# Hybrid decoder layer: the gated linear unit as seven products of quarters, with the merge of its first half placed behind five of the last seven

## The chip, the cores and the metric

The kernel runs on one core of a Trainium2 chip. Its time is the device time of one execution in microseconds (us); lower is better. The engines are PE (TensorE, matrix products), ACT (ScalarE), DVE (VectorE), POOL (GpSimd) and SP (SyncE, which issues most DMA transfers). Each engine works through its own queue in order.

## The reference, cut to what matters

```python
y = s5_ssm(u, ...)                                   # (1, 1040, 1024)
z = jax.nn.gelu(y)
za, zb = jnp.split(z @ w_glu[i], 2, axis=-1)         # w_glu: 1024 x 2048
ssm = za * jax.nn.sigmoid(zb)
merged = (jax.nn.sigmoid(g_att) * rmsnorm(attn, attn_branch_norm[i])
          + jax.nn.sigmoid(g_ssm) * rmsnorm(ssm, ssm_branch_norm[i]))
h = h + merged @ w_out[i]
hn = rmsnorm(h, norm_ffn[i])
gate, up = jnp.split(hn @ w_ffn_in[i], 2, axis=-1)
h = h + (jax.nn.silu(gate) * up) @ w_ffn_out[i]
```

The sequence has 1024 tokens behind 16 prepended ones, the width is 1024, the FFN's inner width 2816. All is float32.

## The kernel before, in words

A float32 product is made of three passes over parts: each operand is split into a high part (cast by ACT to fp32r) and a low part (the difference, on DVE or, for weights read by `w_cols`, on POOL, L104), and `PASSES` gives high x high, high x low, low x high. One "product" below is one matmul instruction of 128 x 128 by 128 x 512.

The stages around the change follow each other. First come the gate projections (`g_unit`), with the attention branch scaled by its gate and written to `pa_d`; beside them DVE runs the scan of the state space branch. Then the z stage: for each of eight blocks of 128 channels three loads (`uty`, `tp`, `ct`, three buffers each), 16 products of 128 columns into `y`, a gelu on ACT into `z`, eight transpositions by PE into `zT`, and the split of these into `zt[h]`, high and low, for the two halves `h` of the tokens. The gated unit follows: for each of eight blocks `f` of output channels and each half, `cols_unit` makes 24 products for `za` and 24 for `zb`; ACT takes the sigmoid, DVE multiplies and applies the gate `gs`, and squares are summed into `acc[h]`. The first half of all blocks, and the second of the first six, come ahead of `merge(0)` in the code; the second halves of blocks 6 and 7 ("late") come after, then `merge(1)`. `merge(h)` makes the root mean square from `acc[h]` (a reduction on PE, `ssq_ssm`; 13 small operations of DVE; four products and a copy, `rsb_ssm`), multiplies the eight blocks, adds the attention branch `mpa` (on POOL) and splits the sum into `mt[h]`. Then `w_out`: two column halves `n`, eight token blocks `b`, 24 products each into `wo`, of which `b` < 4 need `mt[0]` and the others `mt[1]`; DVE adds the residual (`h`, L984), which frees the bank. The FFN behind it already uses seven products of quarters (Strassen's scheme in Winograd's form), with `mixed` making the mixed quarters t2, t1, t4 of its input.

The program is recorded in the order of the code, and the library's scheduler then sorts the instructions of each engine by a timeline it models, within what dependencies and buffers allow. So the order on an engine is not the code's; it is read from the built program. Eight banks hold PE's results, under the tags m (2), s (2), x (3) and q (1).

## Time and profile before

| | |
|---|---|
| median of three runs | 1691.5 us (1687.93 to 1700.41) |
| profiled execution, its own time | 1697.95 us |
| its span in the trace | 1696.2 us |
| mean granted clock of TensorE | 0.975 |
| PE busy | 1586.7 us, 94% |
| DVE busy | 1181.0 us, 70% |
| ACT busy | 695.7 us, 41% |
| POOL busy | 372.4 us, 22% |

The profile is of one execution, so its rows add up to the profiled time and not to the median. The share of PE is a mean over stages: an engine with a low share overall can set the end of one stage. A matmul row's duration is modelled; the distance between the starts of rows tells the pace.

### The profile page before, as it was taken

How to read it: one execution, taken by the hardware profiler on the slowest of the kernel's cores; microseconds unless marked ns; L12 is line 12 of the kernel's file. 1: busy time of each engine (PE TensorE's matmuls, PEld its weight loads, DVE VectorE, ACT ScalarE, POOL GpSimd, SP SyncE). 2: the span in 40 equal slices, each digit the busy share in tenths (PEclk: the TensorE clock that was granted, in tenths of full speed). 3: DMA queues.
4: the chain of work that ended last, by engine and by line, in shares of the span. 5: the costliest groups of instructions: out<-in, count | busy, mean ns of one | idle time of the engine just before them, and what ended most of it. 6: DMA issues, size and time to landing. Idle time of an engine off the chain costs nothing.

```text
span 1696.2 us, 22168 instructions
## 1 busy us (share of the span) xinstructions
PE 1586.7 (94%) x8002; PEld 1318.3 (78%) x8002; DVE 1181.0 (70%) x2280; ACT 695.7 (41%) x1363; POOL 372.4 (22%) x277
## 2 busy tenths in 40 slices
PE   7999888989989999799998897999999999799999
PEld 5788768778867888788887785788888888678787
DVE  7779885999995798732217688865656665399763
ACT  4433425878885421442212333533333333243230
POOL 0000112243321001113323200111111121265441
PEclk9999989999999999999999997999999999999999
DMA  5254442011012874742213341423223331584431
GB/s 190 61 130 133 134 143 74 24 38 45 20 51 60 311 218 131 212 130 75 74 51 104 111 163 57 143 87 106 94 94 116 107 106 56 199 305 159 147 109 75
DMA packets 175359, 196.93 MB, mean 116 GB/s; under 512 B 12769, under 2 KB 125409, under 8 KB 175121
## 3 DMA queue, kind: packets, MB, share of 16 engines
q1 hardware_dynamic: 166736, 183.94, 33.6%
q10 hardware_dynamic: 8288, 11.01, 2.1%
q8 instruction: 63, 1.03, 0.3%
q0 software_dynamic: 224, 0.56, 0.1%
q14 instruction: 48, 0.39, 0.1%
HBM read 140.62 MB, written 54.85 MB: 115 GB/s over the span
## 4 chain that ended last, share of the span: by engine, by line
PE 59%; DVE 14%; DMA 4%; ACT 3%; issue 3%; SPq 0%; POOL 0%; ACTq 0%; DVEq 0%
PE ch_fg L907 6%; PE ch_fu L907 6%; PE ch L907 6%; PE za L122 5%; PE wo L122 5%; PE zb L122 5%; PE si L907 4%; PE g L122 3%; PE th_fg L907 3%; PE th_fu L907 3%; PE q L122 2%; PE si_fg L907 2%; PE si_fu L907 2%; DVE pr L663 1%; DVE cm L207 1%
## 5 line engine op out<-in xcount | busy, mean ns | idle before, releaser
L122 PE MATMUL g<-xn,wh_g 128*128 128x512 f32 x512 | 165.4, 403 | 0.1
L907 PE MATMUL ch<-B,A 128*128 128x512 f32 x528 | 127.2, 398 | 13.8 <-ACT B L1228 7.4
L907 PEld LDWEIGHTS ch<-B,A 128*128 128x128 f32 x528 | 100.7, 192 | 37.7 <-ACT B L1228 7.8
L122 PEld LDWEIGHTS g<-xn,wh_g 128*128 128x128 f32 x512 | 97.2, 192 | 22.7 <-PE s L661 0.3
L122 PE MATMUL q<-wh_q,xn 128*128 128x256 f32 x512 | 105.3, 293 | 5.4 <-ACT qp L620 5.4
L122 PE MATMUL g<-xn,wl_g 128*128 128x512 f32 x256 | 102.2, 399 | 0.0
L907 PE MATMUL si<-B,A 128*128 128x512 f32 x396 | 92.6, 389 | 0.5 <-DVE h2o L911 0.5
L122 PE MATMUL wo<-wh_o,mt 128*128 128x512 f32 x256 | 83.9, 406 | 9.3 <-DVE h L984 4.9
L122 PE MATMUL u<-xn,wh_u 128*128 128x272 f32 (+2 forms) x384 | 92.4, 334 | 0.0
L122 PEld LDWEIGHTS q<-wh_q,xn 128*128 128x128 f32 x512 | 85.1, 196 | 7.0 <-ACT qp L620 5.8
L907 PEld LDWEIGHTS si<-B,A 128*128 128x128 f32 x396 | 74.3, 188 | 16.3 <-issue 0.9
L911 POOL TENSOR_TENSOR a<-c,c_fg 128x512 f32<-128x512 f32 x10 | 15.9, 1586 | 315.0 <-DVE c L911 211.1
L858 DVE TENSOR_TENSOR ssm<-za,zs 128x512 f32<-128x512 f32 x16 | 11.0, 690 | 105.3 <-ACT zs L857 105.3
L1228 ACT CAST A<-rawa 128x1536 fp32r<-128x1536 f32 (+1 forms) x28 | 38.5, 1374 | 99.7 <-issue 49.4
L122 PE MATMUL zb<-zt,wh_zb 128*128 128x512 f32 x256 | 79.3, 390 | 0.0
L122 PE MATMUL za<-zt,wh_za 128*128 128x512 f32 x256 | 79.2, 390 | 0.0
L122 PE MATMUL q<-wl_q,xn 128*128 128x256 f32 x256 | 74.5, 291 | 0.0
L911 DVE TENSOR_TENSOR A<-rawa,A 128x1536 fp32r<-128x1536 f32 (+1 forms) x28 | 65.4, 2334 | 12.5 <-ACT A L1228 12.5
L911 POOL TENSOR_TENSOR B<-t,B 128x1536 fp32r<-128x1536 f32 (+1 forms) x16 | 60.2, 3774 | 54.5 <-ACT B L1228 54.5
L669 ACT ACTIVATE pr<-pr,mn 128x272 f32<-128x272 f32 (+1 forms) x128 | 64.8, 507 | 16.5 <-DVE mn L663 14.0
L122 PEld LDWEIGHTS u<-xn,wh_u 128*128 128x128 f32 x384 | 66.7, 198 | 5.5
L122 PEld LDWEIGHTS wo<-wh_o,mt 128*128 128x128 f32 x256 | 50.0, 196 | 20.5 <-DVE h L984 5.3
(426 smaller groups left out, 4211.6 us busy)
## 6 DMA issues: line engine op xcount, KB each, us to landing
rawa<-act_d SPq DMA_DIRECT2D x21, 768.0 KB
raw_fg<-in_w_ffn_in_dram SPq DMA_DIRECT2D x20, 512.0 KB
raw_fu<-in_w_ffn_in_dram SPq DMA_DIRECT2D x20, 512.0 KB
rawb<-in_w_ffn_out_dram SPq DMA_DIRECT2D x6, 1536.0 KB
act_d<-a SPq DMA_DIRECT2D x33, 256.0 KB
raw_g<-in_w_in_dram SPq DMA_DIRECT2D x16, 512.0 KB
act_d<-c_fg SPq DMA_DIRECT2D x30, 256.0 KB
u_d<-uf SPq DMA_DIRECT2D x64, 65.0 KB
```

The costliest lines, as they stand in the source:

```text
L122: nc.tensor.matmul(o, lhs(kb, a), rhs(kb, b), start=(kb == 0 and i == 0), stop=(kb == n - 1 and i == 2))
L207: nc.vector.tensor_tensor(out=m, in0=v, in1=a[:, 2 * k:2 * k + 2, g0:g0 + 4].unsqueeze(3) .to_broadcast([P, 2, 4, n]), op=ALU.mult)
L663: nc.vector.tensor_tensor_reduce(out=pr[:, h, :n], in0=o[:, :n], in1=mask, scale=1.0, scalar=nsink[:, kv * 4 + h:kv * 4 + h + 1], op0=ALU. ...
L669: nc.scalar.activation(out=pr[:, h, :n], in_=pr[:, h, :n], func=AF.Exp, scale=-1.0, bias=mn[:, h:h + 1], accum_out=den[:, h:h + 1])
L858: nc.vector.tensor_tensor(out=dst, in0=oa, in1=sg, op=ALU.mult)
L907: nc.tensor.matmul(o, lhs(kb, a), rhs(kb, b), start=(first and kb == 0 and i == 0), stop=(kb == n - 1 and i == 2), skip_group_check=not first)
L911: eng.tensor_tensor(out=out, in0=in0, in1=in1, op=op)
L1228: nc.scalar.copy(hi, src)
```

## The change

The unit's output channels are taken in four pairs of blocks `j`, for the gate (`which` = 1, from `zb`) and for the value (`which` = 0, from `za`): eight units. A unit multiplies a 1024 x 256 slab of weights with z; both are cut into quarters, and seven products of 12 matmuls each, of sums of quarters, take the place of eight: 8 x 7 x 12 = 672 matmuls, where 32 x 24 = 768 stood. The names '11', '12', '2', '3', '22', '1', '4' are the seven products, b11, b21, b22 the plain quarters of z, t1 to t4 the mixed ones. The sums of weights, their low parts, the sums of products, the addition in the merge and the sums of squares are all on DVE; POOL has no work left in this part.

The z blocks come in the order 0, 4, 1, 5, 2, 6, 3, 7. When the second of a pair is there, one subtraction on 64 partitions turns the later tokens of the first into the difference, so that its transposition gives t3 at once. The other three mixed quarters are made by `mixed`, which is moved up from the FFN with the functions beside it. To hold two z blocks, the gates' stage keeps one `sg` buffer for two and three `a` for four. The units of the first pair are done together, with '11', '12', '3' and '4' ahead of the products that need t2, t4 and t1. In the last two units five of the seven products come ahead of `merge(0)` in the code, '1' and '4' of both behind it. `mp` is now a ring of seven cells `c`, which also holds the merge's `mpa`.

```diff
...
-        a_ = pool.tile([P, 512], F32, tag="a", bufs=4, name=f"a{f}{h}")
+        a_ = pool.tile([P, 512], F32, tag="a", bufs=3, name=f"a{f}{h}")
...
-        g_unit(i, gp, 2, nc.vector)
+        g_unit(i, gp, 1, nc.vector)
...
+    FOR_B = {"11": "b11", "12": "b21", "2": "t2", "3": "t3", "1": "t1", "22": "t4", "4": "b22"}
+    banks = {}
+    def step_(u, ops, key, first, name):
+        o = banks[u][key]
+        product(o, lambda kb, p: ops[key][p][:, kb, :], lambda kb, p: X[FOR_B[key]][p][:, kb, :], 4, first)
...
+    def mixed(key, a, b, op):
+        for k in (0, 2):
+            t = page(f"{key}f{k}").rearrange("p (k n) -> p k n", k=2)
+            hi, lo = (X[a][p][:, k:k + 2, :].bitcast(F32) for p in range(2))
+            if key == "t2":
+                full[k] = t
+                l2 = page(f"{key}l{k}").rearrange("p (k n) -> p k n", k=2)
+                tt_(t, hi, X[b][0][:, k:k + 2, :].bitcast(F32), op)
+                tt_(l2, lo, X[b][1][:, k:k + 2, :].bitcast(F32), op)
+                tt_(t, t, l2, ALU.add)
+            else:
+                tt_(t, hi, full[k], op)
+                tt_(t, t, lo, ALU.add)
+            split(X[key][0][:, k:k + 2, :], X[key][1][:, k:k + 2, :], t)
+    for key in ("b11", "t3", "b21", "b22"):
+        x_part(key, pool_a)
+    zs = {}
+    def z_turn(blk, keys):
+        for i in range(2):
+            pt = bank(f"zT{blk}{i}", "x")
+            for k in range(4):
+                nc.tensor.transpose(pt[:, k * P:(k + 1) * P], zs[blk][:, T - 1 - (4 * i + k), :], ident)
+            for h in range(2):
+                dst = [X[keys[h]][p][:, blk % 4].rearrange("p (n t) -> p t n", t=T)[:, 4 * i:4 * i + 4, :]
+                       for p in range(2)]
+                split(dst[0], dst[1], pt.rearrange("p (t n) -> p t n", t=4)[:, :, 64 * h:64 * h + 64])
+    for blk in (0, 4, 1, 5, 2, 6, 3, 7):
...
-        z = yp.tile([P, T, P], F32, tag="z", bufs=1, name=f"z{blk}")
+        z = zs[blk] = yp.tile([P, T, P], F32, tag="z", bufs=2, name=f"z{blk}")
...
+        if blk >= 4:
+            late = zs[blk - 4][64:128]
+            tt_(late, z[64:128], late, ALU.subtract)
+            z_turn(blk - 4, ("b11", "t3"))
+            z_turn(blk, ("b21", "b22"))
...
+        def cell(name):
+            return mp.tile([P, 512], F32, tag="c", bufs=7, name=name)
+        def glu_raw(which, j, in_pages=False):
+            a = {}
+            for i in range(2):
+                t = page(f"raw_z{which}{j}{i}") if in_pages else pool_r.tile([P, 1024], F32, tag="raw",
+                                                                             name=f"raw_z{which}{j}{i}")
+                t = t.rearrange("p (k n) -> p k n", k=4)
+                c0 = which * D + 2 * j * P
+                nc.sync.dma_start(out=t, in_=w_glu[i * 512:(i + 1) * 512, c0:c0 + 256]
+                                  .rearrange("(k p) n -> p k n", p=P))
+                for n in range(2):
+                    a[f"{n + 1}{i + 1}"] = t[:, :, n * P:n * P + P]
+            return a
+        def glu_operands(a, keys, name):
+            ops = {}
+            for key in keys:
+                if key == "2":
+                    tt_(a["22"], a["21"], a["22"], ALU.add)
+                    tt_(a["21"], a["11"], a["21"], ALU.subtract)
+                    tt_(a["11"], a["22"], a["11"], ALU.subtract)
+                    tt_(a["12"], a["12"], a["11"], ALU.subtract)
+                    a |= {"1": a["22"], "3": a["21"], "2": a["11"], "4": a["12"]}
+                ops[key] = parts_of(pool_w.tile([P, 2, 512], F32R, tag="w", name=f"wz{key}_{name}"))
+                split(*ops[key], a[key])
+            return ops
+        HALF = {"11": (0, 0), "12": (0, 1), "21": (1, 0), "22": (1, 1)}
...
+        def glu_done(which, j, q, src):
+            n, h = HALF[q]
+            f = 2 * j + n
+            if which:
+                if q not in glu_c[1, j]:
+                    glu_c[1, j][q] = cell(f"zb{f}{h}")
+                nc.scalar.activation(out=glu_c[1, j][q], in_=src, func=AF.Sigmoid)
+                return
+            dst = glu_c[0, j][q]
+            tt_(dst, src, glu_c[1, j][q], ALU.mult)
+            sq = cell(f"sq{f}{h}") if h in acc else mp.tile([P, 512], F32, tag="acc", name=f"acc{h}")
             nc.scalar.activation(out=sq, in_=dst, func=AF.Square)
+            if h in acc:
+                tt_(acc[h], acc[h], sq, ALU.add)
+            else:
+                acc[h] = sq
+            gs = cell(f"gs{f}{h}")
             nc.sync.dma_start(out=gs, in_=sg_d[f][:, 512 * h:512 * h + 512])
             nc.vector.scalar_tensor_tensor(out=dst, in0=dst, scalar=gates[:, 1, f:f + 1], in1=gs,
                                            op0=ALU.mult, op1=ALU.mult)
...
+        def glu_step(which, j, key, ops, apart=False):
+            u = which, j
+            if key == "11":
+                glu_cells(*u)
+            step_(u, ops, key, key in FIRST or (apart and key == "4"), f"z{which}{j}")
+            bk = banks[u]
+            if key == "11":
+                nc.scalar.copy(glu_part(*u, "11"), bk["11"])
+            elif key == "12":
+                c = glu_part(*u, "11")
+                tt_(c, c, bk["12"], ALU.add)
+                glu_done(*u, "11", c)
+            elif key == "2":
+                nc.scalar.copy(glu_part(*u, "21"), bk["2"])
+            elif key == "3":
+                nc.scalar.copy(glu_part(*u, "22"), bk["3"])
+            elif key == "22":
+                c = glu_part(*u, "21")
+                tt_(c, c, bk["22"], ALU.add)
+                glu_done(*u, "21", c)
+            elif key == "1":
+                c = glu_part(*u, "22")
+                tt_(c, c, bk["1"], ALU.add)
+                glu_done(*u, "22", c)
+                if apart:
+                    c = glu_part(*u, "12")
+                    nc.scalar.copy(c, bk["1"])
+                    tt_(c, c, bk["4"], ALU.add)
+                    glu_done(*u, "12", c)
+            elif not apart:
+                glu_done(*u, "12", bk["4"])
...
+        two = ((1, 0), (0, 0))
+        a2 = {u: glu_raw(*u, in_pages=not u[0]) for u in two}
+        ops = {u: {} for u in two}
+        def prepare(*keys):
+            for u in two:
+                ops[u] |= glu_operands(a2[u], keys, f"{u[0]}{u[1]}")
+        prepare("11", "12", "22")
+        for u in two:
+            glu_banks(u, "x" if u[0] else "q")
+        for key in ("t2", "t4", "t1"):
+            x_part(key, pool_x)
+        for keys in (("11", "12"), ("3", "4")):
+            for u in two:
+                for key in keys:
+                    glu_step(*u, key, ops[u], True)
+            if keys[0] == "11":
+                prepare("2", "3", "4")
+        for key, t, a, b, op in (("2", "t2", "t3", "b11", ALU.add), ("22", "t4", "b21", "t2", ALU.subtract),
+                                 ("1", "t1", "b22", "t2", ALU.subtract)):
+            mixed(t, a, b, op)
+            if key == "1":
+                prepare("1")
+            for u in two:
+                glu_step(*u, key, ops[u], True)
         def merge(h):
-            rs = rstd_cols(acc[h], 4, f"ssm{h}", mp)
+            rs = rstd_cols(acc[h], 4, f"ssm{h}", mp, cell(f"rs{h}"))
             for f in range(KB):
                 src = ssm[h, f // 2][:, (f % 2) * 512:(f % 2) * 512 + 512]
-                pa = mp.tile([P, 512], F32, tag="mpa", bufs=4, name=f"mpa{f}{h}")
+                pa = cell(f"mpa{f}{h}")
                 nc.sync.dma_start(out=pa, in_=pa_d[f][:, 512 * h:512 * h + 512])
                 nc.vector.tensor_tensor(out=src, in0=src, in1=rs, op=ALU.mult)
-                nc.gpsimd.tensor_tensor(out=pa, in0=pa, in1=src, op=ALU.add)
+                tt_(pa, pa, src, ALU.add)
                 split(mt[h][0][:, f, 0:512], mt[h][1][:, f, 0:512], pa)
...
+        KEYS = ("11", "12", "2", "3", "22", "1", "4")
+        for j in range(1, 4):
+            ops = {}
+            for which in (1, 0):
+                u = which, j
+                ops[u] = glu_operands(glu_raw(*u), ("11", "12", "22", "2", "3", "1", "4"), f"{which}{j}")
+                glu_banks(u)
+                for key in KEYS[:5 if j == 3 else 7]:
+                    glu_step(*u, key, ops[u])
+        mt = [None, None]
+        for h in range(2):
+            mt[h] = [Rows(f"mt{h}{p}") for p in range(2)]
+            merge(h)
+            if h == 0:
+                for which in (1, 0):
+                    for key in KEYS[5:]:
+                        glu_step(which, 3, key, ops[which, 3])
```

The order of the built programs shows three things that the diff doesn't. The first is on SP in the z stage. `uty`, `tp`, `ct` are a z block's loads, `raw_za`, `raw_zb` and `raw_z` weights of the gated unit, `a` the attention branch. Before:

```order
L100 DMA raw_zb1_0_8000<-in_w_glu_dram 128x8x128
L553 DMA a71_7434<-at_d_76 128x512
L100 DMA raw_za2_0_8124<-in_w_glu_dram 128x8x128
L805 DMA uty3_7597<-u_d_72 128x8x130
L807 DMA tp3_7599<-kl_d_75 128x8x128
L810 DMA ct3_7601<-cp_d_74 128x1024
L100 DMA raw_zb2_0_8130<-in_w_glu_dram 128x8x128
L805 DMA uty4_7647<-u_d_72 128x8x130
```

After:

```order
L871 DMA uty3_7750<-u_d_72 128x8x130
L873 DMA tp3_7752<-kl_d_75 128x8x128
L876 DMA ct3_7754<-cp_d_74 128x1024
L871 DMA uty7_7782<-u_d_72 128x8x130
L873 DMA tp7_7784<-kl_d_75 128x8x128
L876 DMA ct7_7786<-cp_d_74 128x1024
L924 DMA raw_z000_7867<-in_w_glu_dram 128x4x256
L924 DMA raw_z001_7869<-in_w_glu_dram 128x4x256
```

The weights stood between the blocks' loads before; after, the loads of five blocks (three more stand right ahead of these rows) follow each other, and the weights that are loaded in this stage come behind them.

The second is on DVE in the first pair of units, where before only the low parts of `zt` stand, and the first block's sigmoid product. Before:

```order
L200 TENSOR_TENSOR zt01_1_7442<-zT70_7829,zt00_1_7440 128x4x64
L200 TENSOR_TENSOR zt01_1_7442<-zT71_7838,zt00_1_7440 128x4x64
L200 TENSOR_TENSOR zt11_1_7446<-zT70_7829,zt10_1_7444 128x4x64
L200 TENSOR_TENSOR zt11_1_7446<-zT71_7838,zt10_1_7444 128x4x64
L858 TENSOR_TENSOR ssm00_7926<-za00_7876,zs00_7927 128x512
L866 SCALAR_TENSOR_TENSOR ssm00_7926<-ssm00_7926,gates_2271,gs00_7932 128x512
```

After (`t2f`, `t2l`, `t4f`, `t1f` are tiles of `mixed`, `wz_00` and `wz_11` weights of a unit, which and j):

```order
L200 TENSOR_TENSOR wz1_00_8140<-raw_z001_7869,wz1_00_8140 128x512
L818 TENSOR_TENSOR t2f0_8042<-Xt30_7441,Xb110_7439 128x1024
L818 TENSOR_TENSOR t2l0_8043<-Xt31_7442,Xb111_7440 128x1024
L818 TENSOR_TENSOR t2f2_8049<-Xt30_7441,Xb110_7439 128x1024
L818 TENSOR_TENSOR t2l2_8050<-Xt31_7442,Xb111_7440 128x1024
L200 TENSOR_TENSOR wz11_11_8193<-raw_z110_8189,wz11_11_8193 128x512
L818 TENSOR_TENSOR t2f0_8042<-t2f0_8042,t2l0_8043 128x1024
L200 TENSOR_TENSOR wz12_11_8196<-raw_z111_8191,wz12_11_8196 128x512
L818 TENSOR_TENSOR t2f2_8049<-t2f2_8049,t2l2_8050 128x1024
L818 TENSOR_TENSOR t4f0_8083<-Xb210_7443,t2f0_8042 128x1024
L200 TENSOR_TENSOR Xt21_7898<-t2f0_8042,Xt20_7897 128x1024
```

The 1024-wide operations of the mixed quarters have come in, with low parts of the next unit's weights between them.

The third is on PE at the end of the gated unit. `ssq_ssm` is the reduction of `merge(0)`. Before, 61 products of the late blocks stand between it and the first of `wo`:

```order
L122 MATMUL zb61_8895<-zt10_0_7443,wh_zb6_0_8656 128x512
L122 MATMUL zb61_8895<-zt11_0_7445,wh_zb6_0_8656 128x512
L748 MATMUL ssq_ssm0_8791<-ones_92,sq00_7930 128x1 x4
L122 MATMUL zb61_8895<-zt10_0_7443,wl_zb6_0_8657 128x512
L122 MATMUL zb61_8895<-zt10_1_7444,wh_zb6_0_8656 128x512
L122 MATMUL zb61_8895<-zt11_1_7446,wh_zb6_0_8656 128x512
```

After, the last products of the unit ('4', `ch_z`) stand ahead of it, and `wo` right behind:

```order
L814 MATMUL ch_z03_8884<-Xb220_7445,wz4_03_8881 128x512 x2
L814 MATMUL ch_z03_8884<-Xb221_7446,wz4_03_8881 128x512
L814 MATMUL ch_z03_8884<-Xb220_7445,wz4_03_8881 128x512
L748 MATMUL ssq_ssm0_8973<-ones_92,acc0_7960 128x1 x4
L757 MATMUL rsb_ssm00_8997<-ident_87,rs_i_ssm0_8983 128x128 x4
L122 MATMUL wo01_9271<-wh_o0_0_9216,mt00_0_8968 128x512
L122 MATMUL wo01_9271<-wl_o0_0_9217,mt00_0_8968 128x512
L122 MATMUL wo02_9301<-wh_o0_0_9216,mt00_0_8968 128x512
```

The 14 products between the last of '22' (`th_z`) and the reduction are all that is left of the unit; none is behind it. On DVE, the first residual addition stood ahead of the multiplications of `merge(1)` before:

```order
L984 TENSOR_TENSOR h20_9108<-wo00_9111,xr00_9109 128x512
L984 TENSOR_TENSOR h21_9138<-wo01_9141,xr01_9139 128x512
L875 TENSOR_TENSOR ssm10_7985<-ssm10_7985,rsb_ssm1_9013 128x512 x2
L875 TENSOR_TENSOR ssm12_8246<-ssm12_8246,rsb_ssm1_9013 128x512 x2
L875 TENSOR_TENSOR ssm14_8508<-ssm14_8508,rsb_ssm1_9013 128x512 x2
L875 TENSOR_TENSOR ssm16_8920<-ssm16_8920,rsb_ssm1_9013 128x512 x2
L984 TENSOR_TENSOR h22_9168<-wo02_9171,xr02_9169 128x512
L200 TENSOR_TENSOR mt11_0_7862<-mpa01_9020,mt10_0_7860 128x512
```

After, it stands behind the last low part of `mt[1]`:

```order
L200 TENSOR_TENSOR mt11_1_9121<-mpa51_9183,mt10_1_9119 128x512
L200 TENSOR_TENSOR mt11_1_9121<-mpa61_9189,mt10_1_9119 128x512
L818 TENSOR_TENSOR mpa71_9195<-mpa71_9195,ssm13_8888 128x512
L200 TENSOR_TENSOR mt11_1_9121<-mpa71_9195,mt10_1_9119 128x512
L1140 TENSOR_TENSOR h20_9238<-wo00_9241,xr00_9239 128x512
L1140 TENSOR_TENSOR h21_9268<-wo01_9271,xr01_9269 128x512
```

So the bank of the first `wo` comes free only when the merges are done.

## Rows read from the trace of the kernel before

**Rows 1.** Windows by stage: us, each engine's busy time (instructions), clock, DMA, GB/s.

```profile
700.00:730.00 30.00, 26.55 (x233) 25.91 (x231) 19.72 (x39) 20.03 (x39) 0.00 (x0) 1.00 1.02 307
...
730.00:909.00 179.00, 178.91 (x806) 148.13 (x804) 47.60 (x62) 43.18 (x61) 52.73 (x28) 1.00 0.22 68
...
909.00:1015.50 106.50, 97.31 (x437) 80.37 (x438) 76.82 (x164) 32.94 (x65) 19.20 (x13) 0.94 0.42 139
...
1028.00:1062.00 34.00, 19.85 (x60) 13.77 (x58) 33.79 (x41) 14.15 (x21) 0.00 (x0) 0.75 0.24 77
```

**Rows 2.** Timeline of PE, the anchors: start, us, engine line op [idle <-releaser].

```profile
688.03 0.49 PE L823 MATMUL y<-ct,ss 128*128 128x128 f32 x2 [3.82 <-DVE ss L815]
...
729.93 0.71 PE L122 MATMUL za<-zt,wh_za 128*128 128x512 f32 x2
...
835.24 0.62 PE L122 MATMUL zb<-zt,wh_zb 128*128 128x512 f32 x2
...
840.68 0.62 PE L122 MATMUL za<-zt,wh_za 128*128 128x512 f32 x2
...
907.84 0.39 PE L122 MATMUL wo<-wh_o,mt 128*128 128x512 f32 x1
...
913.34 1.22 PE L122 MATMUL wo<-wh_o,mt 128*128 128x512 f32 x2 [4.43 <-DVE mt L200]
...
944.31 0.79 PE L122 MATMUL wo<-wh_o,mt 128*128 128x512 f32 x1 [4.85 <-DVE h L984]
...
1015.47 0.86 PE L907 MATMUL ch_e<-Xb,we 128*128 128x512 f32 x3
```

**Rows 3.** Timeline of DVE, gates, scan and the FFN's mixed quarters.

```profile
644.27 0.69 DVE L554 TENSOR_TENSOR a<-a,rsb_at 128x512 f32<-128x512 f32 x1 [2.13 <-DMA a<-at_d]
...
668.10 0.68 DVE L554 TENSOR_TENSOR a<-a,rsb_at 128x512 f32<-128x512 f32 x1
...
668.70 0.68 DVE L210 TENSOR_TENSOR W<-W,cm 128x512 f32<-128x512 f32 x1
...
669.41 2.77 DVE L207 TENSOR_TENSOR cm<-W,a 128x512 f32<-128x512 f32 x1
...
1030.68 1.22 DVE L911 TENSOR_TENSOR t2f<-Xt,Xb 128x1024 f32<-128x1024 f32 x1
...
1031.82 0.68 DVE L200 TENSOR_TENSOR Xb<-nt_h_b,Xb 128x512 fp32r<-128x512 f32 x1
```

**Rows 4.** SP's timeline, a load of z; then the DMA issues by tile.

```profile
693.10 0.37 SPq L805 DMA_DIRECT2D uty<-u_d  x1
...
uty<-u_d SPq DMA_DIRECT2D x8, 520.0 KB
...
tp<-kl_d SPq DMA_DIRECT2D x8, 512.0 KB
...
ct<-cp_d SPq DMA_DIRECT2D x8, 512.0 KB
```

**Rows 5.** Timeline of ACT: a table load, casts of 256 and 512 columns.

```profile
694.65 1.28 ACT L825 ACT_TABLE_LOAD   x1
...
698.86 1.09 ACT L199 CAST zt<-zT 128x256 fp32r<-128x256 f32 x2 [0.24 <-PE zT L831]
...
906.45 0.62 ACT L199 CAST mt<-mpa 128x512 fp32r<-128x512 f32 x1 [1.09 <-POOL mpa L876]
```

**Rows 6.** Timeline of PE at the beginning of the FFN, behind a gap.

```profile
1036.56 4.59 PE L907 MATMUL th_e<-Xt,wf 128*128 128x512 f32 x10 [3.50 <-DVE wf L200]
...
1040.98 2.49 PE L907 MATMUL ex_e<-Xb,wf 128*128 128x512 f32 x10
```

**Rows 7.** Timeline of DVE in the merges of before.

```profile
893.12 0.16 DVE L751 COPY ms_ssm<-ssq_ssm 128x4 f32<-128x4 f32 x1 [1.14 <-PE ssq_ssm L748]
...
902.27 1.29 DVE L875 TENSOR_TENSOR ssm<-ssm,rsb_ssm 128x512 f32<-128x512 f32 x2 [1.19 <-ACT rsb_ssm L759]
...
934.41 9.24 DVE L875 TENSOR_TENSOR ssm<-ssm,rsb_ssm 128x512 f32<-128x512 f32 x8 [2.86 <-ACT rsb_ssm L759]
```

More of the change, by code (lines that the diff above doesn't have):

```diff
@@ L741, in hybrid_layer_kernel, with rstd_cols @@
     kvp_cm.__exit__(None, None, None)
-    def rstd_cols(acc, nb, name, pool):
+    def rstd_cols(acc, nb, name, pool, rs=None):
         o = bank(f"ssq_{name}", "x")
@@ L798, in hybrid_layer_kernel, with product, tt_ @@
     for i in range(16, 32):
-        g_unit(i, gp, 2, nc.vector)
-    zt = new_a("zt")
-    for blk in range(8):
+        g_unit(i, gp, 1, nc.vector)
+    FIRST = ("11", "12", "3")
+    def product(o, lhs, rhs, n, first):
+        for kb in range(n):
+            for i, (a, b) in enumerate(PASSES):
+                nc.tensor.matmul(o, lhs(kb, a), rhs(kb, b), start=(first and kb == 0 and i == 0),
+                                 stop=(kb == n - 1 and i == 2), skip_group_check=not first)
+    def tt_(out, in0, in1, op, eng=nc.vector):
+        eng.tensor_tensor(out=out, in0=in0, in1=in1, op=op)
@@ new lines, in hybrid_layer_kernel, with x_part, parts_of @@
+    X = {}
+    def x_part(key, pool):
+        X[key] = [half_a(f"X{key}{p}", pool=pool) for p in range(2)]
+    def parts_of(t):
+        return [t[:, p].rearrange("p (k n) -> p k n", k=4) for p in range(2)]
+    FOR_B = {"11": "b11", "12": "b21", "2": "t2", "3": "t3", "1": "t1", "22": "t4", "4": "b22"}
[3 more added lines that the diff above has]
+        product(o, lambda kb, p: ops[key][p][:, kb, :], lambda kb, p: X[FOR_B[key]][p][:, kb, :], 4, first)
@@ L867, in glu_unit, with glu_cells, glu_part @@
                                            op0=ALU.mult, op1=ALU.mult)
+        def glu_cells(which, j):
+            c = glu_c[which, j] = {}
+            if not which:
+                for h in range(2):
+                    ssm[h, j] = page(f"ssm{h}{j}")
+                for q, (n, h) in HALF.items():
+                    c[q] = ssm[h, j][:, 512 * n:512 * n + 512]
+        def glu_part(which, j, q):
+            c = glu_c[which, j]
+            if q not in c:
+                c[q] = cell(f"zc{which}{j}{q}")
+            return c[q]
@@ new lines, in glu_banks @@
+        def glu_banks(u, apart=None):
+            ch, si, th = (bank(f"{n}_z{u[0]}{u[1]}", t) for n, t in (("ch", "m"), ("si", "s"), ("th", "x")))
+            banks[u] = {"11": ch, "12": si, "2": ch, "3": th, "22": th, "1": ch, "4": ch}
+            if apart:
+                banks[u]["4"] = bank(f"ex_z{u[0]}{u[1]}", apart)
+        two = ((1, 0), (0, 0))
[4 more added lines that the diff above has]
+                ops[u] |= glu_operands(a2[u], keys, f"{u[0]}{u[1]}")
@@ L892, in hybrid_layer_kernel @@
-        merge(1)
-    FIRST = ("11", "12", "3")
-    def product(o, lhs, rhs, n, first):
-        for kb in range(n):
-            for i, (a, b) in enumerate(PASSES):
-                nc.tensor.matmul(o, lhs(kb, a), rhs(kb, b), start=(first and kb == 0 and i == 0),
-                                 stop=(kb == n - 1 and i == 2), skip_group_check=not first)
-    def tt_(out, in0, in1, op, eng=nc.vector):
-        eng.tensor_tensor(out=out, in0=in0, in1=in1, op=op)
-    pool_x = front.enter_context(sbuf("pool_x", 6))
@@ L923, in hybrid_layer_kernel @@
+        mt = [None, None]
+        for h in range(2):
+            mt[h] = [Rows(f"mt{h}{p}") for p in range(2)]
[4 more added lines that the diff above has]
+                        glu_step(which, 3, key, ops[which, 3])
     early = {}
@@ L989, in hybrid_layer_kernel @@
                     norm_h(b)
-        FOR_B = {"11": "b11", "12": "b21", "2": "t2", "3": "t3", "1": "t1", "22": "t4", "4": "b22"}
-        banks = {}
-        def step_(u, ops, key, first, name):
-            o = banks[u][key]
-            product(o, lambda kb, p: ops[key][p][:, kb, :], lambda kb, p: X[FOR_B[key]][p][:, kb, :], 4, first)
         for u in range(2):
```

61 lines of the change are left out of this document (4 added, 57 removed).

## The prediction

> **What bounds the kernel now.** I read the windows by stage first. From 730 to 909 us, the gated unit, PE is busy 178.91 of 179.00 us at granted clock 1.00, DVE 47.60, ACT 43.18, GpSimd 52.73 [rows 1]: only PE's queue sets that stretch, and a product taken out shortens it as long as the others keep up. Ahead of it, 700 to 730 (z), the DMA engines are busy all the time at 307 GB/s while PE still has 26.55 of 30 us [rows 1]: transfers and PE end together there. Behind it, 909 to 1015.5, PE loses 9 us and its clock is 0.94 [rows 1]. The PE timeline then gives the anchors: S = 688.03 (first y product, after waiting 3.82 for DVE's `ss`), the first product of the gated unit at 729.93, the first of `w_out` at 907.84, the first behind `w_out` at 1015.47 [rows 2]. I carry the changed kernel from anchor to anchor.
>
> **Products.** Twenty-four products take 840.68 - 835.24 = 5.44 us, 0.2267 each [rows 2]. The order has 768 before and 672 after: 96 x 0.2267 = **-21.8 us**, certain only where PE is the bound.
>
> **Ahead of S (gates and scan).** DVE sets S. GpSimd's lo passes of the first weights go to DVE, with the first sums: 7 operations x 0.60 (successive 512-wide ones start at 668.10 and 668.70) = +4.2. Against it, the operation beside GpSimd's pass took 2.77 us where its like take 0.68 [rows 3]; four such rows in the stretch cost up to 7 us together and go. Three buffers for `a` where there were four: that load is waited for already (2.13 us [rows 3]), and one less can cost up to 4. I take **-2** (-5 to +4).
>
> **z and the hand-over.** Before, S to the first product took 41.9 us [rows 2], with no gap: the weights' loads stood between the y loads and the last y ran straight into `za`. After, SP has five blocks' y loads in a row and the weights of (0,0) behind. A block is 520 + 512 + 512 KB = 1.58 MB [rows 4], five are 7.9 MB, 25.7 us at 307 GB/s. They start when block 0's buffer is free, as the first such load did at 693.10, S + 5 [rows 4], and the last y products run from about S + 32 to S + 36. Then come gelu, the subtraction on 64 partitions (1.14, as the 1024-wide ones at 1030.68 and 1031.82 [rows 3]), and 16 transpositions of the last pair, ending with `zT` at about T = S + 41. In before this chain lay under the first products; now only the 24 products of (1,0)'s '11' and '12' (5.4 us) lie beside it, since (0,0)'s first weights are split behind the last casts and the sigmoid's table: transposition and copy 1.2, six casts at 0.55, DVE's sum 0.9, table 1.28, sigmoid 0.6, cast and lo 1.2 [rows 3, 5], with five hand-overs of nearly 0.5 between engines about 10.9 us. So (0,0) starts at S + 52, as if the unit had started at S + 46.5: **+4.6** (0 to +9).
>
> **First pair of units.** DVE must do some 18 operations of 512 (0.60) and 20 of 1024 (1.14) in the stretch in which PE has 180 products, 40.8 us: 't2' complete at +34, 't4' at +45, 't1' at +49 after T + 10.9, with PE waiting in front of each. The nearest rows are the FFN's own beginning, where the same `mixed` gives PE 19.85 of 34 us at clock 0.75, and ten products take 4.59 us behind a gap where the next ten take 2.49 [rows 1, 6]. Here more products lie in front. I take **+10** for waits and clock (4 to 15; 14 is the FFN's loss, 34 - 19.85). Nothing hides it: these three quarters are in no earlier product.
>
> **The six later units.** 468 products x 0.2267 = 106.1 us of PE; DVE's 121 operations are about 78 us, ACT less. PE stays the bound: +2 for bubbles. The 3.8 us which before's 178 us hold beyond 768 products (907.84 - 729.93 - 174.1: transpositions of zT and the first reduction) lie elsewhere after: **-2** together (-3 to +3).
>
> The last product then comes 9 us earlier counted from S, 11 in all: -21.8 + 4.6 + 10 - 2 - 2.
>
> **The merges.** Here the change gives time back. Before, 61 products (13.8 us) stood behind the first reduction, and `merge(1)` ran under `w_out`. After, by the order, only 14 (3.2 us) are left behind the '22' of (0,3), which completes half 0, all of them ahead of the reduction; everything of `merge(0)` is open to view. From E, the end of that '22': sum, multiplication, square, `acc`, gate and two lo passes on DVE, reduction; from 893.12, the copy of the reduction, to the first multiplication took 9.1 us in before [rows 7]. I get the multiplications from E + 12 and, since multiplication, addition and lo (0.60 each, 1.8 x 8 = 14.4) all lie on DVE with wl_o between, `mt[0]` complete at E + 28.5. The 96 products of the first four `w_out` banks (21.8 us) trail it. `merge(1)` then repeats the chain on the same DVE: its reduction E + 31, multiplications E + 41, `mt[1]` complete E + 55.5, and the first `h` stands behind all of it, so a fifth bank is free only at E + 56. Then 288 products (65.3), and 6.6 for the transpositions of `h` and low clock (before's stage holds 107.6 - 384 x 0.2267 - 9.3 = 11.3 for them): E + 128, which is 125 us after the last product of the unit, where before's 907.84 to 1015.47 took 107.6 [rows 2]: **+17**. Bounds: +8, if the products trail the merges as closely as before's, whose two long waits were 4.43 and 4.85 us [rows 2]; +26, if no product of half 0 runs before `merge(1)`'s sums. GpSimd's addition leaves: 8 multiplications beside it took 9.24 us, 1.16 each [rows 7], and 0.60 without; that is in the sum.
>
> [...] Consecutive 512-wide fp32 operations of DVE start 0.60 us apart while each is shown as 0.68 [rows 3]; I count 0.60. [...]
>
> **Sum.** Against the profiled execution (1697.95, its span 1696.2): -11 + 17 = +6, about 1704; on the median of the three runs, 1691.5, which lies 6.5 below the profiled one, **1697 us**.
>
> **Rivals.** A, *z keeps PE fed*: the loads are no bound, and each pair costs only ACT and DVE, some 9 us, so T = S + 30; -11 on the forecast, 1686. For it: in before the transfers also carried 2 MB of weights in this stretch. Against: the DMA share of 1.02. B, *the later units wait for their weights*, the slower side: the two raw tiles serve one unit, and the next unit's load is issued only when the last of seven operands is split, which waits for one of 8 `w` buffers, that is for a product's end. From '22' of one unit to '12' of the next there are 14 us of products; load, cast, lo and queue need about 8 with DVE free. Beyond 14 each microsecond is PE's; with DVE's queue 10 us behind it costs 4 us in each of six units: +24, 1721. Against it: DVE has 28 us to spare over the 106. C, *only the products show*: mixing and merges find cover that I don't see in the order, 1691.5 - 21.8 = 1670. Against: the 14 products of cover are a fact of the order. That the change removes no product is excluded by the order; that it puts the merge under "the last products" is true of only 14, and that is in the forecast.
>
> **How the numbers follow.** Forecast 0.56, A 0.14, B 0.18, C 0.12. The forecast's own ends, with its bounds not all on one side, are about 1680 and 1715. Leaving out C and half of B, the range is 1676 to 1718. A measurement of this kernel, whose three runs lie 12 us apart, can tell about 1%, 17 us, from no change. Faster by that (under 1674.6) are most of C and a little of the forecast and A: 0.14. Slower (over 1708.4) are most of B and an eighth of the forecast: 0.21. The rest, 0.65.
>
> **What the profile after would show.** PE's products in the unit fewer by 96 at the same 0.2267. S at about 686, the start of (0,0)'s '11' at S + 52 with the DMA share near 1 until S + 32. In the first pair, PE's idle time ended by DVE (`Xt` lo passes, L200) and a granted clock below 1 in slices of it. In the later units, PE busy all through; if rival B holds, idle ended by the loads `raw_z` or by `wz` passes. At the end, two gaps of PE of 10 us and more, ended by DVE's `mt` and `h`, about 125 us from the unit's last product to the FFN's first. The prediction is wrong if those gaps are short (the multiplications start well before E + 12, or the scheduler's `w_out` products cover them), or if DVE's order in the first pair leaves PE waiting under 4 us.

## The result, and the profile after

The changed kernel takes 1713.6 us (median of four runs, 1708.9 to 1719.1) where the kernel before took 1691.8: the ratio is 1.0123 (95% interval 1.0074 to 1.0172). It is slower by 1.2%, some 21 us. The profiled execution took 1708.9, with a span of 1707.1 at a mean clock of 0.967.

PE did less and lost more, as the page's first part says at once (busy time, share of the span, instructions; before, PE was busy 1586.7 us):

```profile
PE 1572.0 (92%) x7906; PEld 1299.7 (76%) x7906; DVE 1262.4 (74%) x2446; ACT 730.5 (43%) x1435; POOL 296.5 (17%) x233
```

The timeline of PE gives the anchors that answer to [rows 2] (S, as in the prediction, is the start of the first y product with its state), and the waits of PE that the argument uses:

```profile
683.86 0.49 PE L889 MATMUL y<-ct,ss 128*128 128x128 f32 x2 [0.49 <-DVE ss L881]
...
724.40 2.35 PE L814 MATMUL ch_z<-Xb,wz 128*128 128x512 f32 x9 [0.73 <-ACT z L891]
...
735.04 0.63 PE L863 MATMUL zT<-ident,z 128*128 128x128 f32 x4 [0.25 <-DVE Xt L200]
...
740.49 3.78 PE L814 MATMUL ch_z<-Xb,wz 128*128 128x512 f32 x8 [2.39 <-ACT wz L199]
...
759.82 0.50 PE L814 MATMUL si_z<-Xb,wz 128*128 128x512 f32 x1 [0.75 <-ACT wz L199]
762.00 4.05 PE L814 MATMUL si_z<-Xb,wz 128*128 128x512 f32 x10 [1.45 <-DVE wz L200]
...
769.95 2.58 PE L814 MATMUL ch_z<-Xt,wz 128*128 128x512 f32 x10 [0.70 <-DVE Xt L200]
...
775.03 0.88 PE L814 MATMUL ch_z<-Xt,wz 128*128 128x512 f32 x2 [2.04 <-ACT Xt L199]
776.23 1.22 PE L814 MATMUL th_z<-Xt,wz 128*128 128x512 f32 x2 [0.31 <-DVE Xt L200]
...
787.58 2.88 PE L814 MATMUL th_z<-Xt,wz 128*128 128x512 f32 x12
...
898.61 3.02 PE L814 MATMUL ch_z<-Xb,wz 128*128 128x512 f32 x12 [2.06 <-DVE ssm L818]
901.46 0.95 PE L748 MATMUL ssq_ssm<-ones,acc 128*128 128x1 f32 x8
907.27 2.08 PE L757 MATMUL rsb_ssm<-ident,rs_i_ssm 128*128 128x128 f32 x8 [4.86 <-DVE rs_i_ssm L159]
916.21 0.80 PE L122 MATMUL wo<-wh_o,mt 128*128 128x512 f32 x1 [6.86 <-ACT mt L199]
...
931.38 0.95 PE L748 MATMUL ssq_ssm<-ones,acc 128*128 128x1 f32 x8
...
958.32 0.77 PE L122 MATMUL wo<-wh_o,mt 128*128 128x512 f32 x1 [14.71 <-DVE h L1140]
...
1030.63 1.56 PE L814 MATMUL ch_e<-Xb,we 128*128 128x512 f32 x6
```

S is 683.86, where before it was 688.03. The unit's first product is at 724.40, the '11' of (0,0) at 740.49 (S + 56.6), the reduction of `merge(0)`, behind the last product, at 901.46 (S + 217.6; before, the last product ended at S + 219.8), and the first product behind `w_out` at 1030.63 (S + 346.8; before S + 327.4). So the unit is 2.2 us shorter and the merges with `w_out` are 129.2 us long instead of 107.6.

The windows by stage (columns as in [rows 1]) cut at these anchors: first pair, later units, merges with `w_out`.

```profile
740.49:787.58 47.09, 41.85 (x156) 32.45 (x157) 43.97 (x54) 20.38 (x32) 0.00 (x0) 0.88 0.10 34
787.58:901.46 113.88, 111.82 (x493) 92.30 (x492) 75.73 (x116) 48.93 (x84) 0.00 (x0) 1.00 0.28 94
901.46:1030.63 129.17, 101.85 (x458) 83.70 (x457) 81.52 (x201) 35.31 (x69) 0.00 (x0) 0.87 0.40 132
```

In the first pair DVE is busy 43.97 of 47.09 us and the clock is 0.88; in the later units PE is busy 111.82 of 113.88 at full clock; behind them the clock is 0.87 and PE idles 27 us.

What PE waits for at the end is on the timeline of DVE:

```profile
896.13 0.69 DVE L818 TENSOR_TENSOR ssm<-ssm,th_z 128x512 f32<-128x512 f32 x1 [6.42 <-PE th_z L814]
...
902.89 0.75 DVE L966 SCALAR_TENSOR_TENSOR ssm<-ssm,gates,gs 128x512 f32<-128x512 f32 x1 [2.34 <-DMA gs<-sg_d]
...
910.00 4.90 DVE L1055 TENSOR_TENSOR ssm<-ssm,rs 128x512 f32<-128x512 f32 x8 [2.79 <-ACT rs L759]
914.83 3.69 DVE L818 TENSOR_TENSOR mpa<-mpa,ssm 128x512 f32<-128x512 f32 x6
...
932.36 0.16 DVE L751 COPY ms_ssm<-ssq_ssm 128x4 f32<-128x4 f32 x1 [4.69 <-PE ssq_ssm L748]
...
941.57 3.10 DVE L1055 TENSOR_TENSOR ssm<-ssm,rs 128x512 f32<-128x512 f32 x5 [6.66 <-ACT rs L759]
...
957.49 0.69 DVE L1140 TENSOR_TENSOR h<-wo,xr 128x512 f32<-128x512 f32 x1 [0.60 <-DMA xr<-in_x_dram]
```

The sum that completes half 0 is at 896.13. Eight multiplications stand ahead of six additions (910.00, 914.83). So the high part of the first block of `mt`, for which PE waits until 916.21, comes behind eight multiplications and one addition, and its low part behind all fourteen operations; `merge(1)` repeats this from 941.57, and the first residual addition is at 957.49, behind it.

From the anchors, the change is worth, counted from S: products -21.8; hand-over +9.3 (56.6 less 5.4 for the 24 products ahead, against 41.9 before); first pair +11.7 (156 products, 35.4 us, took 47.1); later units +2.3 (492 products, 111.5, took 113.9); the 3.8 us that the unit held beside its products before, gone; merges +21.6. That is +19.3. S lies 4.2 us earlier, the FFN's beginning, up to the product that waits for ACT's copy `c_e` (1077.68), takes 0.6 more, and the execution from that product on is 4.9 shorter than in before's profile, so the two profiled executions are 11 us apart and the medians 22. Neither the 4.2 nor the 4.9 is shown to be the change's: in the runs below that leave the program ahead of S as the change has it, S lies between 683.6 and 689.1, and the last part takes 629.4 to 632.1 us in all profiles but three (before's 634.3, x5's 636.2, x9's 635.9); in x8, which is the kernel before but for the residual, it takes 629.5.

### The profile page after: what moved, and what is told of

The parts are those of the page before. It is cut to its first block, busy times and chain, and to the rows that moved or that the text cites. A ratio compares the mean times of both kernels' runs of the same rounds, so it can differ in the third digit from the quotient of the medians.

```text
span 1707.1 us, 22184 instructions
## 1 busy us (share of the span) xinstructions
PE 1572.0 (92%) x7906; PEld 1299.7 (76%) x7906; DVE 1262.4 (74%) x2446; ACT 730.5 (43%) x1435; POOL 296.5 (17%) x233
## 5 line engine op out<-in xcount | busy, mean ns | idle before, releaser
L122 PE MATMUL u<-xn,wl_u 128*128 128x272 f32 (+2 forms) x192 | 63.0, 330 | 0.0
L818 DVE TENSOR_TENSOR h2o<-h2o,ch 128x512 f32<-128x512 f32 x64 | 42.3, 679 | 26.4 <-PE ch L814 24.3
```

The lines of the kernel that those rows point to most:

```text
L122: nc.tensor.matmul(o, lhs(kb, a), rhs(kb, b), start=(kb == 0 and i == 0), stop=(kb == n - 1 and i == 2))
L818: eng.tensor_tensor(out=out, in0=in0, in1=in1, op=op)
```

## The experiments

Each profile was cut at the same anchors. x5, x6 and x7 leave out steps and compute another result; they only price those steps. Counted from S, in us:

| kernel | ratio to before (95%) | '11' of (0,0) | reduction | FFN's first product |
|---|---|---|---|---|
| after | 1.0123 (1.0074 to 1.0172) | 56.6 | 217.6 | 346.8 |
| x1 residual in place | 1.0046 (1.0026 to 1.0066) | 57.1 | 217.8 | 336.8 |
| x2 third product earlier | 1.0109 (1.0078 to 1.0140) | 59.0 | 218.4 | 346.5 |
| x3 merge's addition on GpSimd | 1.0176 (1.0148 to 1.0205) | 56.6 | 220.3 | 355.3 |
| x4 = x1 and x2 | 1.0029 (1.0015 to 1.0043) | 56.7 | 214.8 | 332.4 |
| x5 no late subtraction | 1.0058 (1.0035 to 1.0082) | 51.4 | 207.6 | 333.2 |
| x6 no mixing | 1.0029 (1.0014 to 1.0043) | 56.8 | 205.4 | 330.1 |
| x7 = x4, x5 and x6 | 0.9939 (0.9917 to 0.9961) | 50.8 | 198.9 | 315.7 |
| x8 before, residual in place | 1.0010 (0.9992 to 1.0028) | | | 325.6 |
| x9 = x4 and blocks one by one | 1.0006 (0.9988 to 1.0024) | 56.6 | 215.2 | 324.3 |
| x10 blocks one by one alone | 1.0101 (1.0074 to 1.0129) | 57.3 | 218.1 | 343.9 |
| x11 = x9, three z, two ct | 1.0008 (0.9992 to 1.0023) | 55.2 | 214.4 | 323.3 |
| x12 = x9, three z, one a | 1.0065 (1.0050 to 1.0081) | 62.1 | 219.0 | 328.1 |

**x1.** The residual goes straight into `h2`'s page:

```diff
-                xr = op_.tile([P, 512], F32, tag="xr", name=f"xr{n}{b}")
-                nc.sync.dma_start(out=xr, in_=x[b * P:(b + 1) * P, cols])
+                nc.sync.dma_start(out=h2[b][:, cols], in_=x[b * P:(b + 1) * P, cols])
...
-                nc.vector.tensor_tensor(out=h2[b][:, cols], in0=o, in1=xr, op=ALU.add)
+                nc.vector.tensor_tensor(out=h2[b][:, cols], in0=o, in1=h2[b][:, cols], op=ALU.add)
+                xr = op_.tile([P, 512], F32, tag="xr", name=f"xr{n}{b}")
```

> x is loaded straight into the page of h2, so the residual addition no longer waits for cells that the merge holds. Theory (the merges' loss is mostly the bank release behind merge(1)): PE's wait of 14.7 us ahead of the fifth wo bank falls below 5, the stretch from the unit's last product to the FFN's first from 129 to about 120, the time by 9 (6 to 12), ratio to before about 1.007. Rival (the chain of the merge itself sets the end, since wo of the later tokens needs mt[1] anyway): the wait is named by mt instead and the time falls by less than 3.

PE's restart behind half 0's products, with the first `h` no longer behind `merge(1)` (timeline of PE, x1):

```profile
953.09 0.80 PE L122 MATMUL wo<-wh_o,mt 128*128 128x512 f32 x1 [4.39 <-ACT mt L199]
```

The wait of 14.71 is 4.39 and now named by `mt`; the merges' stretch is 118.9 us, and the ratio falls by 0.8%, 13 us. Half of the merges' loss was the bank release. The pool of `xr` opens in the code where the pool of the merge's cells closes, and its loads were issued only at the end of `merge(1)` (SP's timeline, changed kernel):

```profile
954.93 18.73 SPq L1137 DMA_DIRECT2D xr<-in_x_dram  x8
```

In x1 the loads into `h2`'s page begin at 921.32, so the addition that frees a bank no longer stands behind `merge(1)`.

**x2.** `KEYS` with "3" ahead of "2".

> The products of a later unit in the order 11, 12, 3, 2, 22, 1, 4: the copy that the '22' waits for lies under '2', and by the order 37 products instead of 14 stand between the '22' of (0,3) and the reduction. Theory (too little cover for merge(0)): the waits ahead of rsb_ssm and of the first wo together, 11.7 us, fall by about 5, and the time by 5. Rival (merge(1) sets the end, whatever covers merge(0)): under 2.

```profile
911.25 1.01 PE L757 MATMUL rsb_ssm<-ident,rs_i_ssm 128*128 128x128 f32 x3 [3.04 <-DVE rs_i_ssm L159]
920.19 0.80 PE L122 MATMUL wo<-wh_o,mt 128*128 128x512 f32 x1 [6.86 <-ACT mt L199]
...
962.83 0.76 PE L122 MATMUL wo<-wh_o,mt 128*128 128x512 f32 x1 [14.72 <-DVE h L1140]
```

The first wait is 3.04 where it was 4.86 with 2.06 ahead, and the other two are as they were. Counted from S the FFN begins only 0.3 us earlier, but this profile lost 2.4 us ahead of '11' (59.0 against 56.6), with a wait for a load that the other one doesn't have:

```profile
720.63 0.46 PE L889 MATMUL y<-ct,ss 128*128 128x128 f32 x2 [1.95 <-DMA ct<-cp_d]
```

From '11' to the FFN it is 287.5 us against 290.2, 2.7 less, and the ratio says 2.4 less with overlapping intervals: nearer to the rival (under 2) than to the theory (5). The 37 products cover only the way to the reduction, which PE's order has behind them all; the chain from there to `mt` stays in view.

**x3.** `tt_(pa, pa, src, ALU.add, nc.gpsimd)` in `merge`.

> The addition of the merge back on GpSimd, as before the change. Theory (the lost cover and the bank release are the cause, not the engine of the addition): within 4 us of the changed kernel, since 16 additions of 0.60 leave DVE, but its multiplications beside GpSimd take 1.16 each and GpSimd needs 1.7 for each addition. Rival (DVE's extra additions stretch the merges): 8 us or more faster.

The eight multiplications of `merge(0)` (timeline of DVE, x3), which took 4.90 us in the changed kernel:

```profile
915.14 11.32 DVE L1055 TENSOR_TENSOR ssm<-ssm,rs 128x512 f32<-128x512 f32 x8 [2.79 <-ACT rs L759]
```

Neither: the profile is 8.5 us slower, and the ratio 0.5% higher, though its interval overlaps that of the change. The eight take 1.4 us each on the mean instead of 0.60, more than the 1.16 of [rows 7]. Taken one by one, the first two run alone, 0.60 apart; behind them multiplications and GpSimd's additions begin by turns, each kind 1.67 us apart (timelines of DVE and of GpSimd, x3):

```profile
918.02 1.75 DVE L1055 TENSOR_TENSOR ssm<-ssm,rs 128x512 f32<-128x512 f32 x1
...
919.18 1.72 POOL L818 TENSOR_TENSOR mpa<-mpa,ssm 128x512 f32<-128x512 f32 x1
...
919.70 1.76 DVE L1055 TENSOR_TENSOR ssm<-ssm,rs 128x512 f32<-128x512 f32 x1
```

So each 1.67 us hold one multiplication and one addition, where a multiplication alone follows the one before by 0.60 and the shortest addition of this run took 1.26; what makes them take turns, no run shows. By the profile, that the change took the addition off GpSimd was a gain.

**x4.** x1 and x2 together.

> x loaded into h2's page and '3' ahead of '2' together. Theory: the two waits are one after the other, so the gains add: 14 us faster than the changed kernel, ratio to before about 1.004. Rival (one chain of DVE work under both): no better than the better of the two alone.

```profile
911.34 0.80 PE L122 MATMUL wo<-wh_o,mt 128*128 128x512 f32 x1 [6.87 <-ACT mt L199]
...
943.38 0.79 PE L122 MATMUL wo<-wh_o,mt 128*128 128x512 f32 x1 [4.39 <-ACT mt L199]
```

16 us faster than the change in ratio; against x1 the FFN begins 4.4 us earlier (332.4), 4.0 counted from '11'. So the cover that x2 adds is worth something with the bank release repaired as without it (2.7); the difference of the two is too small for one profile each.

**x5.** The loop over `range(8)`, `z_turn` of each block as it is there, and neither `late` nor its subtraction.

> z's blocks in their plain order, each turned as soon as it is there; the subtraction that makes t3 ahead of the transposition is left out, so the third product takes a plain quarter and the result is another. Theory (pairing the blocks puts one pair's turning, the table load and the weights' casts in view at the hand-over, 9 us): the '11' of (0,0) starts 47 to 49 us after the first y with its state, instead of 56.6, and the time falls by 7 to 10. Rival (the weights of (0,0), whose load waits for z's memory, set the start whatever the order of z): the start moves by less than 2.

```profile
727.57 3.02 PE L814 MATMUL ch_z<-Xb,wz 128*128 128x512 f32 x12
...
737.20 2.58 PE L814 MATMUL ch_z<-Xb,wz 128*128 128x512 f32 x10 [0.72 <-DVE wz L200]
```

The unit's first product follows the last y product at once and '11' of (0,0) is at S + 51.4: 5.2 us earlier, between theory (8 to 10) and rival. The order of z and the subtraction were taken out together, so the run doesn't tell their shares. The reduction comes 10 us earlier, since the wait of 2.06 at the unit's end and part of the first pair's loss went too. In time it is 11 us, 0.65%.

**x6.** `mixed` is left out in the unit, and t2, t4, t1 are other names of b11, b21, b22 there.

> The mixed quarters t2, t4 and t1 are not made in the gated unit; the products read plain quarters in their place, so 14 additions, 6 casts and 6 low parts of 1024 columns and PE's waits for them are gone, and the result is another. Theory (DVE's mixing opens the first pair): from the '11' of (0,0) 156 products take 36 to 38 us instead of 47.1, the time falls by 10 to 12. Rival (the low parts and sums of the first weights, all on DVE, hold the first pair too): under 6.

The 156 products of the first pair (window, x6):

```profile
742.07:779.10 37.03, 37.03 (x156) 30.50 (x157) 25.44 (x40) 17.36 (x31) 0.00 (x0) 0.95 0.23 77
```

They take 37.03 us instead of 47.09, with PE busy throughout: the theory's number. The run takes DVE's additions and low parts and ACT's casts out together, and doesn't part them. In time it is 16 us; the rest is the 2.06 at the unit's end and 4.5 in the merges' stretch (124.7). Of these 3.0 are shorter waits of PE, 3.04 us where the change has 4.86 and 13.56 where it has 14.71; why they are shorter, this experiment doesn't explain.

**x7.** x4, x5 and x6 together.

> x loaded into h2's page, '3' ahead of '2', plain order of z without the subtraction, and no mixing, together (another result). Theory: the costs lie at three places that don't share cover, so they add: the measured 16 of the two orders, 9 of the hand-over and 11 of the mixing give about 1677, ratio to before 0.992 (0.989 to 0.996), which is the gain by the products less what the merges still cost. Rival (they share one cover, DVE's): 0.998 or more.

The ratio, 0.9939, is within the theory's bounds: with the three taken out the saving of products shows. The merges' stretch is still 116.8 us. The reduction is 18.7 us earlier, where the single ones make 25 (10.0, 12.2, 2.8): some 6 are shared.

**x8.** The edit of x1 in the kernel before.

> The kernel before with x loaded straight into h2's page. Theory: its first additions stood ahead of merge(1) already and one wait of 4.85 us is named by h, so it gains 0 to 4 us, ratio 0.998 to 1.0; what the load into the page repairs is the change's own loss. Rival (the residual's tiles hold back both kernels alike): 8 us or more.

No change: the interval holds 1. The bank release was the changed kernel's own loss.

**x9 and x10.** The multiplication's result goes into the free `acc` tile, so that DVE works block by block; in x9 on top of x4, in x10 alone:

```diff
-                nc.vector.tensor_tensor(out=src, in0=src, in1=rs, op=ALU.mult)
-                tt_(pa, pa, src, ALU.add)
+                tt_(acc[h], src, rs, ALU.mult)
+                tt_(pa, pa, acc[h], ALU.add)
```

> Both orders (x into h2's page, '3' ahead of '2'), and each multiplication of the merge written into the one acc tile that the addition behind it reads, so that DVE does multiplication, addition and low part block by block instead of eight multiplications first. Theory (PE waits in both merges for the first block of mt, which stands behind eight multiplications): the waits of 6.9 and 4.4 us named by mt shrink by 4 each, the stretch from the unit's end to the FFN from 117.6 to 110 to 113, the time by 5 to 8 against both orders alone, ratio to before 0.998 to 1.000. Rival (the last block of mt sets the end and comes when it came, as DVE's work is the same): under 2, ratio 1.002 to 1.003.

> The changed kernel with the merge's multiplications written into the acc tile, block by block, and nothing else. Theory: the bank release behind merge(1) still sets PE's restart, so only the first wait (6.9 us) shrinks and the last low part comes as before: 0 to 3 us faster. Rival (the grouping of multiplications is the merges' cost by itself): 6 us or more.

```profile
912.22 0.79 PE L122 MATMUL wo<-wh_o,mt 128*128 128x512 f32 x1 [2.78 <-ACT mt L199]
...
940.61 0.79 PE L122 MATMUL wo<-wh_o,mt 128*128 128x512 f32 x1 [2.55 <-ACT mt L199]
```

The waits for `mt` in x9 fall from 6.87 and 4.39 to 2.78 and 2.55, and the stretch is 109.0 us, below what was forecast. The FFN begins 8.1 us earlier than in x4; the ratio, 1.0006, is a little above the theory's upper end and its interval overlaps x4's. x9 is level with the kernel before: of the versions tried that compute the reference's output none is faster than it. In x10 the first wait falls too, but the bank release grows:

```profile
960.79 0.77 PE L122 MATMUL wo<-wh_o,mt 128*128 128x512 f32 x1 [17.55 <-DVE h L1140]
```

17.55 us where it was 14.71. PE began earlier and ran out of banks earlier; 2.9 us are left in the profile, as the theory had it (3.7 by the ratios, whose intervals overlap).

**x11 and x12.** `bufs=3` for z, paid for with `bufs=2` for `ct` (x11) or `bufs=1` for `a` (x12), on top of x9.

> As the orders and pairs run, with three z buffers where the changed kernel has two, paid for by two ct buffers where it has three. Theory (the hand-over is long because the gelu of block 7 waits for the transpositions of the pair ahead to give back its buffer): the '11' of (0,0) starts 51 to 54 us after S instead of 56.6, the time falls by 3 to 5 against orders and pairs, ratio to before 0.997 to 0.999. Rival (the turning and casts of the last pair on ACT and DVE set it, with any number of buffers, or the later ct loads take the gain back): 56 us or more, the time within 2.

> The same three z buffers, paid for by one a buffer where the changed kernel has three. Theory: the '11' again 51 to 54 us after S; S itself comes 3 to 8 us later, because each a load, some 3 us, now waits for the write of the one before it, so the time is 0 to 4 us above the run with two ct. Rival (a is loaded in time with one buffer, as DVE is the bound ahead of S): S unmoved within the 5 us by which it scatters, and the time equal to that of two ct.

In x11 '11' is at S + 55.2, 1.3 earlier than in x9, and the time is the same: that theory of the hand-over falls, or the waits that came in its stead took the gain, 1.98 us for a `ct` load among them: the gelu of block 7 follows its y products at once here (728.30), but these end at S + 43 instead of S + 38. The run doesn't tell the two apart. In x12 S is 697.6, 8 us past all others, '11' at S + 62.1, and the ratio up by 0.6%, 10 us: one `a` buffer costs more than either expectation, because gates that no longer fit ahead of S lie in the z stage, where PE now waits for them:

```profile
704.98 0.80 PE L887 MATMUL y<-tp,uty 128*128 128x128 f32 x2 [2.97 <-ACT sg L548]
```

## Why the prediction came out as it did

**The sum.** Forecast 1697 in a range of 1676 to 1718, with 0.65 on "within 1%"; measured 1713.6, 1.2% slower, which had 0.21, so the likeliest case ended one class too low. Its mechanism, a saving of products eaten at three places, is what the runs show; the three terms of loss were all too small. Counted from S the terms make +7.8 and the profiles +19.3. Of these 11.5 us, 4.7 are the hand-over's, 1.7 the first pair's, 0.5 the later units' and 4.6 the merges'; the rest of the 16.6 between 1697 and the median lies outside these terms, where S and the FFN scatter. That 1713.6 is in the range owes something to its width: the hand-over lies just past its own bound (9) and the merges in the upper half of theirs, and the upper end of 1718 was drawn with half of rival B in it, which did not happen.

**Products, -21.8.** Held: in the later units 492 products took 113.9 us. x7 shows the saving when the rest is taken away.

**Ahead of S, -2.** S at 683.9 says -4.2, but it scatters by 5 with the same program, so this term can't be told from nothing. One reading in it was off: of rows stretched beside GpSimd's passes the trace of before has three ahead of S (655.65, 669.41 and 681.96), 5.6 us together, not four and 7.

**Hand-over, +4.6 (0 to 9); measured +9.3.** The step that failed is T. I had the last transposition at S + 41, five us behind the last y product. That product was at S + 38 instead of S + 36, but the pair's last `zT` is at 735.04, S + 51. The chain behind T, forecast at 10.9, took 5.5, so two errors of 10 and 5 us partly cancelled. The trace of before could have warned: its own last `zT` is at 738.68, S + 50.7, while products of the unit ran around it from 729.93 on (timeline of PE, before):

```profile
738.68 1.04 PE L831 MATMUL zT<-ident,z 128*128 128x128 f32 x8
```

ACT's timeline (changed kernel) shows one delay ahead of T: block 7's gelu is at 729.00, behind a cast that waits for the pair ahead, 7 us after its y products:

```profile
728.59 0.61 ACT L199 CAST Xb<-zT 128x256 fp32r<-128x256 f32 x1 [1.64 <-PE zT L863]
729.00 1.12 ACT L891 ACTIVATE z<-y 128x512 f32<-128x512 f32 x2
...
738.00 1.28 ACT L954 ACT_TABLE_LOAD   x1
739.30 0.63 ACT L954 ACTIVATE zc<-zc 128x512 f32<-128x512 f32 x1
739.83 1.64 ACT L199 CAST wz<-raw_z 128x512 fp32r<-128x512 f32 x3
```

DVE's timeline (changed kernel) has what takes over from that cast and that gelu, and the sum in the chain behind T:

```profile
729.24 0.66 DVE L200 TENSOR_TENSOR Xb<-zT,Xb 128x256 fp32r<-128x256 f32 x1 [1.41 <-ACT Xb L199]
730.15 1.22 DVE L818 TENSOR_TENSOR z<-z,z 64x1024 f32<-64x1024 f32 x1 [0.25 <-ACT z L891]
...
738.54 0.68 DVE L818 TENSOR_TENSOR zc<-zc,si_z 128x512 f32<-128x512 f32 x1
```

DVE begins 0.04 us behind the end of the cast (728.59 and 0.61) and 0.03 behind that of the gelu (729.00 and 1.12), and the sum takes 0.68. The 10.9 had five hand-overs of nearly 0.5 and 0.9 for the sum: both were my estimates, and no run shows them.

x5, with the plain order of z and no subtraction, gives back 5.2 of the 9.3, nearly all of it at T (S + 46.2). What holds the rest stays open: x11's third z buffer moved little, and the table load of 1.28 us and the sigmoid of 0.63 (738.00, 739.30) stand ahead of the weights' casts (739.83), the load as in x3 (741.82). The transfers were not the bound that I took them for: PE waited for `ct` or `tp` less than 1 us at any place in the z stage of this profile (1.95 in x2's), and the DMA engines' share from S to the unit's first product (second column from the right) was 0.78, not near 1:

```profile
683.86:724.40 40.54, 35.33 (x298) 33.75 (x299) 26.28 (x48) 21.41 (x41) 0.00 (x0) 1.00 0.78 227
```

In that rival A was right; its T = S + 30 was not.

**First pair, +10; measured +11.7.** The size was right, and x6 shows the cause: without the mixing, 10 of the 11.7 are gone. Its parts differ from the forecast's: PE idles 5.2 us (41.85 busy of 47.09), of which 2.2 end with weights' parts (`wz`, 759.82 and 762.00) and 3.1 with mixed quarters, and the other 6.5 are slower products at a mean clock of 0.88. DVE ends the low parts of t2, t4 and t1 29, 37 and 40 us behind that '11', where the prediction had +34, +45 and +49 (timeline of DVE, changed kernel):

```profile
768.67 1.22 DVE L200 TENSOR_TENSOR Xt<-t2f,Xt 128x1024 fp32r<-128x1024 f32 x1
...
776.69 1.22 DVE L200 TENSOR_TENSOR Xt<-t4f,Xt 128x1024 fp32r<-128x1024 f32 x1
777.83 2.35 DVE L200 TENSOR_TENSOR Xt<-t1f,Xt 128x1024 fp32r<-128x1024 f32 x2
```

So the quarters came sooner than forecast, the clock cost more than the waits, and that the sum is near +10 is partly luck.

**Later units, -2; measured -1.5** (2.3 - 3.8). Rival B, weights that come late, is out: up to the last 12 products PE waited nowhere in them.

**Merges, +17 (8 to 26); measured +21.6.** With E, the end of the '22' of (0,3), at 896.1, the chain was right link by link, but each came late: the multiplications at E + 14, not 12, behind a wait of 2.34 us for `gs`; `mt[0]` complete at E + 30, not 28.5; the second reduction at E + 35, not 31, and its multiplications at E + 45, not 41, since PE's order has both small products behind those of `wo` (DVE waits 4.69 and 6.66 us for them, 932.36 and 941.57); the restart at E + 62, not 56. Of the two gaps of 10 us and more that the prediction looked for, one is 14.71, ended by `h`; the other is two, 4.86 and 6.86, with the products of `rsb_ssm` between them. The step that failed is the place of the second reduction in PE's order, behind products of `wo`, which I costed at nothing. And I counted the residual's place behind `merge(1)` as part of one chain where x1, x4 and x9 show three costs that can be taken away one by one: the bank release (10 us), the cover (4 with the release repaired, 2.7 without) and DVE's grouping of multiplications (8).

**DVE's price.** The 0.60 that the forecast counts for an operation of 512 and the 1.14 for one of 1024 held: six additions take 3.69 us (914.83 above), 0.60 apart, and two low parts of 1024 take 2.35 (777.83 above) where one alone takes 1.22, 1.13 apart. So the loss lies in the places above, and not in the price of DVE's operations.
